# The last expert's tail in a one-core decoder layer: the final weight piece cut by rows, its products in a row, its sums and stores on two engines

## The chip, the cores and the metric

The kernel runs on one core of a Trainium2 chip, as one program from one launch. The metric is the device time in microseconds (us), the median of the runs. The engines are named TensorE (PE in the profile, PEld for its weight loads), VectorE (DVE), ScalarE (ACT), GpSimd (POOL) and SyncE (SP). SyncE issues nearly all DMAs here.

## The reference, cut to what matters

The layer is an RMS norm, one input projection, a state-space mixer and a stick-breaking attention side by side, their merge, an output projection and a residual add; then a mixture of 32 experts over 256 tokens of width 2048. All of it is fp32. The change lies in the last expert of the mixture:

```
D_MODEL = 2048; SEQ = 256; N_EXPERTS = 32; D_FF_EXPERT = 512
# top-1 group of 8 experts, top-2 experts in it; combine[token, e] is the gate, 0 where not chosen
for e in range(N_EXPERTS):
    hid = jax.nn.silu(t @ w_gate[e]) * (t @ w_up[e])
    out = out + combine[:, e:e + 1] * (hid @ w_down[e])
return x + out
```

## The kernel before, in words

After the first part (projection, mixers, merge, router) the experts are worked through, four to a group q (eight groups). Each expert has 32 slots for tokens. `gather` selects the tokens of the four experts by a one-hot matrix (128 slots), `gate_up` computes gate and up products and the transposed hidden activations `hT` of one expert, `down` multiplies them by the down weights, and `scatter` brings the four experts' results back to the tokens and adds them to `accv`, a tile of 128 x 2 x 2048 in SBUF: t = 0 and 1 are the two halves of the 256 tokens, n = 0 to 3 the four quarters of 512 columns.

An expert's weights come in six pieces of 2 MiB, each a tile `ew` of 128 rows by 4096 numbers: four pieces of gate and up (`wgu`), two of down (`wd`; piece 4 for the output columns 0 to 1023, piece 5 for 1024 to 2047). `load_piece` (line 867) issues them on SyncE's queue in the order of `pieces`, into a ring of buffers, well ahead of their use. For experts 30 and 31 the order is changed: all of their gate and up pieces, then (30,4), (31,4), (30,5), (31,5). The last, (31,5), is loaded in two halves of its columns (`LSPLIT` = 512, line 883), so that the first half can be used while the second is on its way.

`down(e, hT, dn, c0, cw)` (line 1137) makes `cw` output columns from `c0` on: matmuls with 32 slots as rows, four column groups of the array at a time, into a PSUM tile `dn`, and then four copies by ScalarE into `Y4` (rows 32i to 32i+31 for expert i of the group; `Y4` is a part of the tile shown as XY). `scatter(q, n, ts)` (line 1152) takes, for each t, a PSUM tile, one matmul of `SC` (the gates, transposed; shown as sc) with `Y4`, one VectorE add into `accv`, and in the last group a store of that part of the output by SyncE. A matmul of fp32 shows as two entries in the trace for 128x512.

The program's order is the order in the code (a manual schedule), engine by engine; waits between engines are semaphores put in by the framework. PSUM tiles come from three pools: `acc` with four banks, `bga` and `bgb` with two each. `keep_busy(n)` issues n transposes into an `acc` tile that nobody reads.

Behind the last store is a loop over experts with more than 32 tokens (line 1198); in the run shown its body isn't entered. All engines read its count (`oli`) and branch over the body.

The tail, in order (lines 1174 to 1189): `gate_up` of experts 30 and 31, `down` of both for columns 0 to 1023, `scatter` of n = 0 and 1, `down` of 30 for 1024 to 2047, `down` of 31 for 1024 to 1535, `scatter` of n = 2 for t = 0, `down` of 31 for 1536 to 2047, `scatter` of n = 2 for t = 1, and of n = 3.

Of the kernel before, what the change touches and what calls it, by code (L numbers as in the profile page):

```python
# [13 lines left out]
OP = mybir.AluOpType  # L14
# [3 lines left out]
P = 128  # L18
# [19 lines left out]
TAILB = (24, 24, 0, 0)  # L38
LSPLIT = 512
# [43 lines left out]
def hybrid_block(ctx, tc, A, out):  # L83
    nc = tc.nc
    load = {"vec": 0.0, "act": 0.0, "pe": 0.0}
    vec = Meter(nc.vector, load, "vec")
    act = Meter(nc.scalar, load, "act")
    pe = Meter(nc.tensor, load, "pe")
    sp, pool = nc.sync, nc.gpsimd
# [3 lines left out]
    def unit(i, shape, dt, name):  # L93
        return U[i].tile(shape, dt, name=name, tag="u")
# [13 lines left out]
    def acc_tile(name="acc"):  # L108
        return pacc.tile([P, 512], F32, name=name, tag="acc")

    def bg_tile(k):
        return pbg.tile([P, 512], F32, name="bg" + "ab"[k], tag="bg" + "ab"[k])
# [46 lines left out]
    ident = cp.tile([P, P], F32, name="ident")  # L159
# [109 lines left out]
    S = {}  # L269
# [137 lines left out]
    for b, s in turns:  # L407
        src, nk, begin, mm, fin = blocks[b]
# [452 lines left out]
    pieces = [(e, i) for e in range(NE - 2) for i in range(6)]  # L861
# [5 lines left out]
    def load_piece():  # L867
        n = nextp[0]
        if n >= len(pieces):
            return  # L870
        j = n % 11 if n < 22 else (n - 22) % 10
        j += n >= 22 and j > 5
        if used[0] <= held.get(j, -1):
            return
        held[j] = n
        e, i = pieces[n]
        tl = ring[j].tile([P, 4, 1024], F32, name="ew", tag="u")
        src = A["wgu"][e][:, 4 * i:4 * i + 4] if i < 4 else A["wd"][e][:, 4 * i - 16:4 * i - 12]
        if n < 7:
            for k in range(4):  # L880
                ahead.append(lambda k=k: sp.dma_start(tl[:, k], src[:, k]))
        else:
            for c0, cw in (((0, 1024),) if n < len(pieces) - 1 else ((0, LSPLIT), (LSPLIT, 1024 - LSPLIT))):
                sp.dma_start(tl[:, :, c0:c0 + cw], src[:, :, c0:c0 + cw])
        ptile[e, i] = tl
        nextp[0] += 1

# [30 lines left out]
    for i in range(nsub):  # L918
        prog["step"] = i
        src, s, nk, begin, mm, fin = subs[i]  # L920
# [14 lines left out]
        for g in (gens[:1] if i < HOLD else list(gens)):  # L935
            while rest.get(g, 0) <= i:
                if load["pe"] > pe0 + BURST or load["vec"] > load["pe"] + SLACK or load["act"] > load["pe"] + SLACK:
                    break
                c = next(g, None)
# [13 lines left out]
        if i >= first_out - X2_AT - 8 and (i % 2 == 0 or 0 <= i - first_out + X2_AT < 4):  # L953
            if not ahead and nextp[0] < 7:
                load_piece()
            if ahead:
                ahead.pop(0)()
        if i == nsub - 4:
            load_piece()
# [10 lines left out]
    def keep_busy(n):  # L970
        ps = acc_tile()
        for _ in range(n):
            pe.transpose(ps[:, 0:P], ident, ident)
# [90 lines left out]
    Y4 = XY[:, 1].rearrange("p a b -> p (a b)")  # L1064


    SC = [None, None]
# [41 lines left out]
    def gate_up(e, gen):  # L1109
        q, i = divmod(e, 4)  # L1110
        gu = acc_tile()
        for k4 in range(4):
            next(gen, None)
            if k4 == (1 if e == 0 else 0):
                next(gen, None)
            if e >= NE - 2:
                keep_busy(24)
            w = ptile[e, k4]
            for kk in range(4):
                k = 4 * k4 + kk  # L1120
                for j in range(4):
                    pe.matmul(gu[32 * j:32 * j + 32, 0:T], XB[:, k, 32 * i:32 * i + 32], w[:, kk, T * j:T * j + T],
                              start=(k == 0), stop=(k == 15), tile_position=(0, 32 * j))
            used[0] += 1
            load_piece()
        for _ in gen:
            pass
        sg = rt.tile([P, P], F32, name="sg", tag=f"sg{e % 2}")
        act.activation(sg, gu[:, 0:P], AF.Silu)
        vec.tensor_tensor(sg, sg, gu[:, P:T], op=OP.mult)  # L1130
        ht = bg_tile(1)
        pe.transpose(ht[:, 0:P], sg, ident)
        hT = rt.tile([P, P], F32, name="hT", tag=f"hT{e % 2}")
        act.copy(hT, ht[:, 0:P])
        return hT

    def down(e, hT, dn, c0, cw):
        i = e % 4
        w = ptile[e, 4 + c0 // 1024]
        n4 = cw // 4  # L1140
        for j in range(4):
            for c in range(4):
                x0 = c0 % 1024 + n4 * c
                pe.matmul(dn[32 * c:32 * c + 32, c0 // 4:c0 // 4 + n4], hT[:, 32 * j:32 * j + 32],
                          w[:, j, x0:x0 + n4], start=(j == 0), stop=(j == 3), tile_position=(0, 32 * c))
        if (c0 + cw) % 1024 == 0:
            used[0] += 1
            load_piece()
        for c in range(4):
            act.copy(Y4[32 * i:32 * i + 32, c0 + n4 * c:c0 + n4 * c + n4], dn[32 * c:32 * c + 32, c0 // 4:c0 // 4 + n4])  # L1150

    def scatter(q, n, ts=(0, 1)):
        if q == 0 and n == 0:
            S["acc"] = unit(3, [P, 2, D], F32, "accv")
        accv = S["acc"]
        c = slice(512 * n, 512 * n + 512)
        for t in ts:
            ps = acc_tile()
            pe.matmul(ps, SC[q % 2][:, P * t:P * t + P], Y4[:, c], start=True, stop=True)
            vec.tensor_tensor(accv[:, t, c], (x2 if q == 0 else accv)[:, t, c], ps, op=OP.add)  # L1160
            if q == NE // 4 - 1:
                sp.dma_start(out[t][:, c], accv[:, t, c])
# [3 lines left out]
    for e in range(NE - 2):  # L1166
        hT = gate_up(e, gather(e // 4) if e % 4 == 0 else iter(()))
        dn = acc_tile()
        for c0 in (0, 1024):
            down(e, hT, dn, c0, 1024)  # L1170
            if e % 4 == 3:
                for n in range(c0 // 512, c0 // 512 + 2):
                    scatter(e // 4, n)
    pair = [(e, gate_up(e, iter(())), acc_tile()) for e in (NE - 2, NE - 1)]
    q = NE // 4 - 1
    keep_busy(TAILB[0])
    down(*pair[0], 0, 1024)
    keep_busy(TAILB[1])
    down(*pair[1], 0, 1024)
    scatter(q, 0)  # L1180
    scatter(q, 1)
    keep_busy(TAILB[2])
    down(*pair[0], 1024, 1024)
    keep_busy(TAILB[3])
    down(*pair[1], 1024, LSPLIT)
    scatter(q, 2, (0,))
    down(*pair[1], 1024 + LSPLIT, 1024 - LSPLIT)
    scatter(q, 2, (1,))
    scatter(q, 3)


    accv = S["acc"]
# [5 lines left out]
    with tc.For_i(0, novr) as it:  # L1198
        er = nc.values_load(oli[0:1, bass.ds(it + 1, 1)], min_val=0, max_val=NE - 1)
        gp = [acc_tile() for _ in range(4)]  # L1200
        for k4 in range(4):
# [8 lines left out]
            for i in range(4):  # L1210
                k = 4 * k4 + i
                for t in range(2):
                    for hf in range(2):
                        pe.matmul(gp[2 * t + hf], XO[:, k, P * t:P * t + P], WO[k4][:, i, 512 * hf:512 * hf + 512],
                                  start=(k == 0), stop=(k == 15))
# [12 lines left out]
        for t in range(2):  # L1228
            for n in range(4):
                ps = acc_tile()  # L1230
                for j in range(4):
                    pe.matmul(ps, hOT[:, j, P * t:P * t + P], WO[n // 2][:, j, 512 * (n % 2):512 * (n % 2) + 512],
                              start=(j == 0), stop=(j == 3))
                c = slice(512 * n, 512 * n + 512)
# [56 lines left out]
```

## Time and profile before

| what | value |
|---|---|
| median of 3 runs | 1557.23 us (1555.97 to 1557.52) |
| the profiled execution, its own time | 1555.73 us |
| its span (first to last instruction) | 1553.9 us |
| mean granted TensorE clock | 0.923 of full |
| PE busy | 1252.9 us (81%) |
| PEld busy | 856.7 us (55%) |
| DVE busy | 540.5 us (35%) |
| ACT busy | 451.1 us (29%) |
| DMA | 516.91 MB, mean 333 GB/s |

Times in the rows are us from the start of the span unless marked ns. A timeline row gives the start, the time from the first start to the last end, engine, line, operation, out<-in, shapes and xcount, and in brackets the idle time before it with what ended it. Because of a helper that records every operation, all compute rows have line 77; the tiles tell them apart. Matmuls overlap, so a row of several is shorter than their sum, and the ends of matmuls are modelled. In the rows by stretch the columns are: the stretch, its length, then for PE, PEld, DVE, ACT and POOL the busy us and (x) the number of instructions, then the granted TensorE clock as a share, the busy share of the 16 DMA engines and GB/s. A name with a q (SPq, PEldq) is an engine's sequencer, which waits, branches and issues DMAs.

### The profile page before, as it was taken

To read this page: it belongs to the slowest core of one execution; us is meant where nothing else is said; L and a number is where in the kernel's file an instruction comes from. 1 tells how busy PE (TensorE), PEld (TensorE's weight loads), DVE (VectorE), ACT (ScalarE), POOL (GpSimd) and SP (SyncE) were. 2 spreads that over 40 slices of the span, in tenths; PEclk is the share of its full clock that TensorE was granted. 3 is DMA by queue.
4 is the path that set the end of the run, shared out by engine and by line. 5 is a ranking of instruction groups with operands and counts; after the bars stand their busy time and mean duration, and the time that the engine had idled before them with its cause. 6 is when DMAs were issued, how large, how long until landed. Compare 5 with 4: busy or idle time off the path is not lost. (4 is left out here: it accounts for less than half of the span.)

```text
span 1553.9 us, 25147 instructions
## 1 busy us (share of the span) xinstructions
PE 1252.9 (81%) x10662; PEld 856.7 (55%) x10662; DVE 540.5 (35%) x1344; ACT 451.1 (29%) x768; POOL 48.1 (3%) x105
## 2 busy tenths in 40 slices
PE   9999999999999999878558558557657657656697
PEld 8888888888878888644224224224223324323364
DVE  6746788898866744302002002002002002002001
ACT  5654577544454444121101100110110110110101
POOL 6500000000000000000000000000000000000000
PEclk9999999999999999999789779888888889879899
DMA  7645555566658877999999999999999999999996
GB/s 259 200 148 161 178 163 162 162 191 191 190 189 287 273 270 245 382 427 428 427 426 428 426 427 427 427 427 428 426 428 427 427 427 427 427 427 427 427 427 259
DMA packets 65108, 516.91 MB, mean 333 GB/s; under 512 B 7905, under 2 KB 8161, under 8 KB 41441
## 3 DMA queue, kind: packets, MB, share of 16 engines
q1 hardware_dynamic: 64704, 515.21, 84.4%
q8 instruction: 86, 1.41, 0.4%
q14 instruction: 30, 0.24, 0.0%
q10 hardware_dynamic: 288, 0.06, 0.0%
HBM read 513.14 MB, written 2.10 MB: 332 GB/s over the span
## 5 line engine op out<-in xcount | busy, mean ns | idle before, releaser
L77 PE MATMUL acc<-ew,XY 128*32 128x256 f32 x4096 | 309.1, 455 | 169.9 <-DMA ew<-wgu 169.8
L77 PEld LDWEIGHTS acc<-ew,XY 128*32 128x32 f32 x4096 | 142.3, 126 | 320.7 <-DMA ew<-wgu 189.1
L77 DVE TENSOR_TENSOR wl<-raw,wh 128x1024 fp32r<-128x1024 f32 (+1 forms) x201 | 244.1, 1217 | 140.6 <-ACT wh L77 139.3
L77 ACT CAST wh<-raw 128x1024 fp32r<-128x1024 f32 x199 | 208.6, 1053 | 179.0 <-PE acc L77 113.7
L77 DVE TENSOR_TENSOR sg<-sg,acc 128x128 f32<-128x128 f32 x32 | 9.2, 288 | 660.2 <-ACT sg L77 660.2
L77 PE MATMUL acc<-ew,hT 128*32 128x256 f32 (+1 forms) x2080 | 149.2, 436 | 71.3 <-DMA ew<-wd 39.4
L77 ACT COPY XY<-acc 32x256 f32<-32x256 f32 (+1 forms) x260 | 93.7, 360 | 209.8 <-PE acc L77 207.3
L77 PEld LDWEIGHTS acc<-ew,hT 128*32 128x32 f32 x2080 | 73.6, 123 | 138.3 <-issue 54.8
L77 PE MATMUL acc<-wh,xh 128*128 128x512 f32 x512 | 144.8, 399 | 1.1 <-DVE wh L77 0.8
L77 PE MATMUL acc<-wh,xl 128*128 128x512 f32 x512 | 140.3, 391 | 0.0
L77 PE MATMUL acc<-wl,xh 128*128 128x512 f32 x512 | 140.0, 390 | 0.0
L77 ACT ACTIVATE sg<-acc 128x128 f32<-128x128 f32 x32 | 8.9, 278 | 416.0 <-PE acc L77 416.0
L77 PEld LDWEIGHTS acc<-wh,xl 128*128 128x128 f32 x512 | 96.6, 189 | 20.6
L77 PEld LDWEIGHTS acc<-wl,xh 128*128 128x128 f32 x512 | 96.5, 189 | 20.3
L77 PEld LDWEIGHTS acc<-wh,xh 128*128 128x128 f32 x512 | 93.4, 189 | 20.2 <-issue 1.2
L77 DVE TENSOR_TENSOR Vs<-Vs,prod 128x32 f32<-128x32 f32 x508 | 76.9, 222 | 0.0
L77 PE MATMUL acc<-XY,sc 128*128 128x512 f32 x128 | 61.9, 624 | 14.7 <-ACT XY L77 14.5
L77 PE MATMUL bga<-SL,x 128*128 128x128 f32 x512 | 63.5, 280 | 10.3 <-DVE SL L77 10.3
L77 PEld LDWEIGHTS bga<-SL,x 128*128 128x128 f32 x512 | 59.0, 192 | 22.9 <-DVE SL L77 15.9
L77 DVE TENSOR_TENSOR accv<-accv,acc 128x512 f32<-128x512 f32 x56 | 38.5, 688 | 79.9 <-PE acc L77 79.9
L77 PE MATMUL acc<-wh,m 128*128 128x512 f32 x256 | 64.6, 392 | 0.0
L77 DVE TENSOR_TENSOR prod<-Vs,coef 128x64 f32<-128x64 f32 x254 | 56.1, 263 | 0.0
(222 smaller groups left out, 972.5 us busy)
## 6 DMA issues: line engine op xcount, KB each, us to landing
ew<-wgu SPq DMA_DIRECT2D x123, 2048.0 KB, 39.3
ew<-wd SPq DMA_DIRECT2D x61, 2048.0 KB, 39.4
raw<-win SPq DMA_DIRECT2D x127, 512.0 KB, 4.2
raw<-wout SPq DMA_DIRECT2D x32, 512.0 KB, 4.2
ew<-wgu SPq DMA_DIRECT2D x20, 512.0 KB, 5.6
raw<-wba SPq DMA_DIRECT2D x16, 512.0 KB, 4.5
raw<-wbs SPq DMA_DIRECT2D x16, 512.0 KB, 4.8
raw<-wglu SPq DMA_DIRECT2D x8, 512.0 KB, 5.5
```

Source lines behind the costliest of these rows:

```text
L77: return f(out, *args, **kw)
```

## The change

The last weight piece is loaded as rows 0 to 119 and rows 120 to 127, over all its columns, instead of as two column halves. The tail after `scatter` of n = 1 is rewritten. `down` of expert 30 is as it was. Then, for n = 2 and 3, a tile `ends[n, 1]` is opened in PSUM with a matmul of the identity and `accv[:, 1]`, which puts the sum so far of the second token half there. The two products of expert 31 (512 columns each) follow in a row; the first goes into its tile as before and is copied by VectorE, the second goes into another tile and is copied by ScalarE. Last come four scatter matmuls. For t = 0 VectorE adds the result to `accv` and SyncE stores it; for t = 1 the matmul adds onto what the identity matmul left in PSUM, ScalarE copies it to `accv`, and ScalarE's own queue stores it. The two calls of `keep_busy` that go were of length 0.

```diff
         else:
-            for c0, cw in (((0, 1024),) if n < len(pieces) - 1 else ((0, LSPLIT), (LSPLIT, 1024 - LSPLIT))):
-                sp.dma_start(tl[:, :, c0:c0 + cw], src[:, :, c0:c0 + cw])
+
+            for r in ((slice(0, P),) if n < len(pieces) - 1 else (slice(0, 120), slice(120, P))):
+                sp.dma_start(tl[r], src[r])
...
-    def down(e, hT, dn, c0, cw):
+    def down(e, hT, dn, c0, cw, copy=act.copy):
...
-            act.copy(Y4[32 * i:32 * i + 32, c0 + n4 * c:c0 + n4 * c + n4], dn[32 * c:32 * c + 32, c0 // 4:c0 // 4 + n4])
+            copy(Y4[32 * i:32 * i + 32, c0 + n4 * c:c0 + n4 * c + n4], dn[32 * c:32 * c + 32, c0 // 4:c0 // 4 + n4])
...
-    keep_busy(TAILB[2])
     down(*pair[0], 1024, 1024)
-    keep_busy(TAILB[3])
-    down(*pair[1], 1024, LSPLIT)
-    scatter(q, 2, (0,))
-    down(*pair[1], 1024 + LSPLIT, 1024 - LSPLIT)
-    scatter(q, 2, (1,))
-    scatter(q, 3)
+
+    accv = S["acc"]
+    ends = {}
+    for n in (2, 3):
+        ends[n, 0] = bg_tile(0)
+        ends[n, 1] = acc_tile()
+        pe.matmul(ends[n, 1], ident, accv[:, 1, 512 * n:512 * n + 512], start=True, stop=False)
+    e, hT, dn = pair[1]
+    down(e, hT, dn, 1024, 512, vec.tensor_copy)
+    down(e, hT, acc_tile(), 1536, 512)
+    for n in (2, 3):
+        c = slice(512 * n, 512 * n + 512)
+        for t in range(2):
+            pe.matmul(ends[n, t], SC[q % 2][:, P * t:P * t + P], Y4[:, c], start=not t, stop=True)
+            if t:
+                act.copy(accv[:, t, c], ends[n, t])
+                nc.scalar.dma_start(out[t][:, c], accv[:, t, c])
+            else:
+                vec.tensor_tensor(accv[:, t, c], accv[:, t, c], ends[n, t], op=OP.add)
+                sp.dma_start(out[t][:, c], accv[:, t, c])
```

TensorE at the end of the program, before: the row of 32x256 is `down` of expert 30, the rows of 32x128 are expert 31, the rows `acc<-XY,sc` are scatter matmuls; what an instruction waits for stands in brackets (DMAHW is a load's landing).

```order
L77 MATMUL acc<-ew,hT 32x256 x15
L77 MATMUL acc<-ew,hT 32x128 [waits DMAHW4_49]
L77 MATMUL acc<-ew,hT 32x128 x15
L77 MATMUL acc<-XY,sc 128x512 [waits DVE_49,Activation_49]
L77 MATMUL acc<-ew,hT 32x128 [waits DMAHW5_49]
L77 MATMUL acc<-ew,hT 32x128 x15
L77 MATMUL acc<-XY,sc 128x512 [waits DVE_49]
L77 MATMUL acc<-XY,sc 128x512 [waits Activation_49]
L77 MATMUL acc<-XY,sc 128x512 [waits DVE_49]
```

The same place now, with the identity matmuls as `acc<-accv,ident`:

```order
L77 MATMUL acc<-ew,hT 32x256 x15
L77 MATMUL acc<-accv,ident 128x512 [waits DVE_49] x2
L77 MATMUL acc<-ew,hT 32x128 [waits DMAHW5_49,DMAHW4_49]
L77 MATMUL acc<-ew,hT 32x128 x15
L77 MATMUL acc<-ew,hT 32x128 [waits Activation_49]
L77 MATMUL acc<-ew,hT 32x128 x15
L77 MATMUL bga<-XY,sc 128x512 [waits DVE_49]
L77 MATMUL acc<-XY,sc 128x512
L77 MATMUL bga<-XY,sc 128x512 [waits Activation_49]
L77 MATMUL acc<-XY,sc 128x512
```

Both products of expert 31 have moved ahead of every scatter matmul of n = 2 and 3, two identity matmuls stand before them, and the first of them waits for both loads.

ScalarE at the end of the program now, from its copies for expert 30 on (32x256); before, eight copies of 32x128 stood between these and the read of `oli`:

```order
L77 COPY XY<-acc 32x256 x3
L77 COPY XY<-acc 32x128 [waits PE_49]
L77 COPY XY<-acc 32x128 x3
L77 COPY accv<-acc 128x512 [waits DMAHW5_49,DMAHW3_49,DMAHW6_49,DMAHW0_49,PE_49]
L1200 DMA out<-accv 128x512 [waits DMAHW3_49,Activation_49]
L77 COPY accv<-acc 128x512 [waits PE_49]
L1200 DMA out<-accv 128x512 [waits DMAHW5_49,Activation_49]
L1211 TENSOR_LOAD oli [waits DVE_49]
```

Four of the small copies have gone to VectorE, and two large copies and two stores have come to ScalarE ahead of its read of `oli`; VectorE has two adds fewer in turn.

## Rows read from the trace of the kernel before

**Rows 1.** Chain of waits in order of time: start, us, what.
```profile
1545.19 2.00 PE acc L77 x4
...
1547.21 0.69 DVE accv L77
```
**Rows 2.** Busy time by stretch; columns as described in the section on the profile.
```profile
1500.00:1520.00 20.00, 19.10 (x230) 14.58 (x229) 0.29 (x1) 0.54 (x2) 0.00 (x0) 1.00 1.01 427
...
1531.00:1532.00 1.00, 1.00 (x27) 0.73 (x20) 0.00 (x0) 0.00 (x0) 0.00 (x0) 1.00 0.50 213
...
1542.00:1543.00 1.00, 1.00 (x6) 0.24 (x10) 0.00 (x0) 0.00 (x0) 0.00 (x0) 1.00 0.19 57
```
**Rows 3.** Timeline of SP, issues: piece before the last, second half of the last.
```profile
1495.91 0.33 SPq L884 DMA_DIRECT2D ew<-wd  x1
...
1505.64 7.34 SPq L884 DMA_DIRECT2D ew<-wd  x1
```
**Rows 4.** DMA issues, the same two in order: xcount, KB, us to landing.
```profile
ew<-wd SPq DMA_DIRECT2D x1, 2048.0 KB, 39.4
...
ew<-wd SPq DMA_DIRECT2D x1, 1024.0 KB, 34.9
```
**Rows 5.** Timeline of PE from expert 30's second down product on (the first two overlap).
```profile
1537.27 1.93 PE L77 MATMUL acc<-ew,hT 128*32 128x256 f32 x32
...
1537.27 2.81 PE L77 MATMUL acc<-ew,hT 128*32 128x256 f32 x64
1541.88 1.12 PE L77 MATMUL acc<-XY,sc 128*128 128x512 f32 x2 [1.80 <-ACT XY L77]
1542.93 1.08 PE L77 MATMUL acc<-ew,hT 128*32 128x128 f32 x32
1543.94 3.23 PE L77 MATMUL acc<-XY,sc 128*128 128x512 f32 x6
...
1545.19 1.98 PE L77 MATMUL acc<-XY,sc 128*128 128x512 f32 x4
```
**Rows 6.** Timeline of ACT, the copies for expert 31's two halves.
```profile
1540.77 1.06 ACT L77 COPY XY<-acc 32x128 f32<-32x128 f32 x4
...
1544.08 1.06 ACT L77 COPY XY<-acc 32x128 f32<-32x128 f32 x4 [2.26 <-PE acc L77]
```
**Rows 7.** Timeline of DVE, three of the last group's eight adds.
```profile
1537.37 0.69 DVE L77 TENSOR_TENSOR accv<-accv,acc 128x512 f32<-128x512 f32 x1 [0.17 <-PE acc L77]
...
1546.36 0.69 DVE L77 TENSOR_TENSOR accv<-accv,acc 128x512 f32<-128x512 f32 x1 [0.56 <-PE acc L77]
1547.21 0.69 DVE L77 TENSOR_TENSOR accv<-accv,acc 128x512 f32<-128x512 f32 x1 [0.17 <-PE acc L77]
```
**Rows 8.** Groups of instructions by form: count | busy us, mean ns | idle before.
```profile
L77 ACT COPY xt<-bga 128x512 f32<-128x512 f32 x8 | 4.7, 583 | 17.8 <-PE bga L77 17.8
...
L77 DVE TENSOR_TENSOR sg<-sg,acc 128x128 f32<-128x128 f32 x32 | 9.2, 288 | 660.2 <-ACT sg L77 660.2
...
L77 DVE COPY OV<-bgb 32x1 f32<-32x1 f32 x1 | 0.1, 147 | 0.1
```
**Rows 9.** Timeline: the last store's issue on SP; an issue on ACT.
```profile
1547.93 0.33 SPq L1162 DMA_DIRECT2D out<-accv  x1
...
1.09 0.43 ACTq L425 DMA_DIRECT2D g<-g  x1
```
**Rows 10.** DMA issues, the store of 1543.75 and the last: KB, us to landing.
```profile
out<-accv SPq DMA_DIRECT2D x1, 256.0 KB, 2.5
...
out<-accv SPq DMA_DIRECT2D x1, 256.0 KB, 4.1
```
**Rows 11.** Line 1198, the branch and its waits: ns min/median/max, first and last start.
```profile
L1198 PEldq COMPARE_BRANCH  x1: 4417/4417/4417, 1547.5 to 1547.5; - x1
...
L1198 SPq EVENT_SEMAPHORE  x2: 17/17/17, 1552.0 to 1552.1; - x2
...
L1198 ACTq COMPARE_BRANCH  x3: 38/38/54, 1544.7 to 1552.4; - x3
```

## The prediction

> **What bounds the kernel now.** I read the stretches of the span first. The whole second half is paced by loading: 427 GB/s with every DMA engine busy [rows 2], and this change leaves all of that alone. It touches the last load and what follows it, so only the last 20 us of 1553.9 are at stake. The chain of waits, read next, ends in four matmuls and one add into accv at 1547.21 [rows 1]; behind them stand the last store and the end of the program.
>
> The last loads: the piece before the last is issued at 1495.91 and lands 39.4 us later, at 1535.3; the second half of the last piece goes out at 1505.64 and lands after 34.9, at 1540.5 [rows 3, 4]. From 1531 on the loads run at half the rate (share 0.50, 213 GB/s) [rows 2]: half of the DMA engines are done, the other half carries the tail.
>
> On TensorE [rows 5], `down` of expert 30 (32 matmuls of 256 columns) starts at 1537.27, 2.0 us after its weights landed, since the previous sums stood before it. The first half of expert 31 follows directly (x64, 2.81 us). Then TensorE idles until 1541.88, 1.80 us, for ScalarE, whose last four copies start at 1540.77 [rows 6]. So the order is: one sum, the second half of `down` at 1542.93 (2.4 us after its weights), ScalarE's copies at 1544.08, and sums from 1545.19. What ends last here is the ping-pong of TensorE and ScalarE, and not the DMA. [...]
>
> Behind the last add (1547.21 + 0.69 = 1547.90) two things run side by side. The last store is issued at 1547.93 and lands 4.1 us later, at 1552.0, where an earlier one took 2.5 [rows 9, 10]. TensorE's branch over the overflow loop starts at 1547.5 and takes 4.417 us, to 1551.9; SyncE's wait for the landing ends at 1552.0 [rows 11]. Both end together, and 1.9 us of closing follow.
>
> **The change part by part.**
>
> *120 and 8 rows.* One DMA engine's share of a 2 MiB piece takes 2.097 MB / 427 GB/s = 4.91 us [rows 2], so a last piece in whole rows is in at 1535.3 + 4.91 = 1540.2 if the 120 rows spread evenly, against 1540.5. One more row on a late engine costs 4.91 / 8 = 0.61 us, which gives 1540.8. I keep both. What is lost is the early half: both products now wait for the whole piece, behind which the rest of TensorE's work is queued.
> [...]
>
> *Two identity matmuls of accv.* A product of 128x512 is two entries; from the pair at 1541.88 to the next work at 1542.93 are 1.05 us, and a second pair adds 1.98 - 1.12 = 0.86, in all 1.91 [rows 5]. They begin when `down` of expert 30 is through: 1537.27 + 2.81 - 1.08 = 1539.00. Their two banks were read by VectorE's adds, the last at 1537.37 + 0.69 = 1538.06 [rows 7], so they do not wait. They end at 1540.91. Cost: 1.91 us of TensorE, but they stand where it idles now and cover the load (1540.2 to 1540.8). That cover is thin: a load later than 1540.8 is paid in full.
>
> *Products in a row, two banks.* The first 32 matmuls of expert 31 now start at 1540.91, not 1539.00; the second 32 follow 2.81 - 1.93 = 0.88 later [rows 5], at 1541.79 instead of 1542.93. TensorE is through with them 1.01 after that (1542.93 to 1543.94), at 1542.80.
>
> *Copies by two engines.* A copy starts 1.15 us after the first of its 32 matmuls (1542.93 to 1544.08) [rows 5, 6]. VectorE thus begins at 1542.06. No row has a VectorE copy of 32x128 out of PSUM: a copy of 32x1 takes 147 ns, an operation of 128x128 on PSUM 288 [rows 8]; ScalarE's takes 1.06 / 4 = 265. I take 250, nearest to these last: four are 1.0 us, to 1543.06 (bounds 1542.65 and 1543.21). ScalarE starts the other four at 1542.94 and ends at 1544.00.
>
> *The four sums.* They start 0.05 after the copies (1545.14 to 1545.19), at 1543.11; bounds 1542.80, where TensorE gets free, and 1543.26. The third needs ScalarE's copies (1544.00), but its turn comes at 1544.9. A sum is there 1.17 after its start (1545.19 to 1546.36), each further one 0.85 later (to 1547.21) [rows 5, 7]. The last is there at 1543.11 + 1.17 + 3 x 0.855 = 1546.85, against 1547.21: **0.36 us earlier** (0.21 to 0.67). The gain is small because four sums now stand behind the last copies where two did: they start 2.08 earlier, and the two more give 1.71 back.
>
> *Half of the adds in PSUM.* For t=1, ScalarE's copy of 128x512 (583 ns) stands in for VectorE's add (0.69) [rows 7, 8]. Last copy: 1546.85 + 0.58 = 1547.43 against 1547.90, 0.47 earlier.
>
> *Two store queues.* An issue holds SyncE 0.33 us, and one on ScalarE took 0.43 [rows 9]; the results come 0.85 apart, so no store waits for another's issue and I count nothing. ScalarE's first copy into accv also waits for two loads and for two of the first four stores; their adds were over by 1538.06 [rows 7], some 7 us before, so I count nothing there either. Its register load and branch move behind its last issue, to about 1547.9, ahead of TensorE's end.
>
> *The end.* TensorE's branch moves by the same 0.36: 1547.5 - 0.36 + 4.42 = 1551.6. The last store lands at 1547.46 + 2.5 = 1550.0, or 1551.6 if it is held as now (4.1). Either way the end moves by 0.36. The profiled execution took 1555.73, 1.83 beyond its span; it becomes 1555.4. The median of the three runs, 1557.23, lies 1.5 above it, and on that I put the forecast: **1556.9 us**. That is 0.02%; less than 0.2%, some 3.1 us, can't be told from no change here.
>
> **The rivals.**
>
> *The 120 rows spread badly (slower).* No transfer of before has a row count other than 128. If the 120 rows go to eight engines, 15 each, and those are the late ones, with one of the 8 rows on top, their queue ends at 1535.3 + 16 x 0.61 = 1545.1. TensorE, free at 1540.9, waits for 4.2 us of it, since both products need all rows; less the 0.36 that is +3.8: 1561.0. It decides from a landing after 1540.9, and shows above 0.2% from one after 1544.4. For it: half of the engines do run late. Against it: if the eight are the early half, done by 1531, nothing is lost. Chance 0.06.
> [...]
>
> *TensorE's branch gets short, or the store's delay goes (faster than forecast).* The 4.417 us are one event, and ScalarE's branch at the same line takes 38 to 54 ns [rows 11]. If TensorE's vanishes, the store at 1550.0 ends the kernel, 2.0 earlier: 1555.2. The loop body that it jumps over is unchanged, which speaks against it. Chance 0.08.
>
> *ScalarE becomes the last.* It now issues the last store and branches after it. Should its branch take what TensorE's does, 1547.43 + 0.43 + 4.42 = 1552.3, 0.4 later than TensorE's 1551.9 now, and its register load comes on top: about +0.7, 1557.9. Before, its branch takes 38 to 54 ns [rows 11], so 0.08.
>
> **How the numbers follow.** The forecast has 0.78. Its own range is 1556.6 to 1557.0 by the bounds, and 1555.3 to 1557.6 with the spread of the runs (1555.97 to 1557.52). Low end: the short branch with a fast run, 1554.9; high end: the ScalarE case with a slow one, 1558.6. What is left out is the bad spread and runs off in either direction. Slower by over 0.2%: 0.06 of the first rival and 0.01 of drift; faster by that much: no case reaches it, 0.03 for drift; within 0.2%: 0.90.
>
> **What would show it.** Identity matmuls right behind `down` of expert 30, before 1539.1; no wait on DMA at the 64 matmuls of expert 31; VectorE copies of about 250 ns; the four sums in a row without a gap, the last 3.7 us after the first starts; TensorE's branch again some 4.4 us long and within 0.2 us of the last landing. I am wrong if TensorE waits for the last piece, if the VectorE copies take over 300 ns, or if another wait closes the program.

## The result, and the profile after

The changed kernel takes 1567.16 us (median of 4 runs, 1565.35 to 1569.55) against 1556.69 us: ratio 1.0066, 95% interval 1.0054 to 1.0079. It is slower by about 10.5 us, where the prediction said no change (1556.9). The profiled execution took 1567.27 us with a span of 1565.6 (before: 1555.73 and 1553.9).

The stretches of the span, columns as in [rows 2], show it first:

```profile
1500.00:1520.00 20.00, 18.97 (x230) 14.38 (x227) 0.29 (x1) 0.55 (x2) 0.00 (x0) 1.00 1.01 426
...
1527.00:1534.00 7.00, 5.61 (x67) 4.64 (x66) 0.00 (x0) 1.45 (x4) 0.00 (x0) 1.00 0.95 211
...
1539.00:1543.00 4.00, 3.16 (x33) 1.29 (x25) 0.00 (x0) 0.81 (x3) 0.00 (x0) 0.50 0.51 135
...
1545.00:1547.00 2.00, 2.00 (x4) 0.77 (x3) 0.93 (x2) 0.00 (x0) 0.00 (x0) 0.50 0.56 193
```

From 1500 to 1520 us the rate is as before (426 GB/s with all engines busy). From 1527 to 1534 the DMA engines are still busy (0.95) but move half as much, 211 GB/s. In [rows 2] a rate of 213 came with a share of 0.50: there half of the engines were done, here all work at half speed. A packet of these loads is 16,384 B in the trace (one row), so 16 engines x that x share / rate is the time of one: 0.62 us at first, 1.18 us here. The trace's own records of these packets have the same means, 0.62 and 1.18 us.

The issues of the first down piece of expert 31, still 128 rows, and of the 120 rows (KB, us to landing):

```profile
ew<-wd SPq DMA_DIRECT2D x1, 2048.0 KB, 45.1
...
ew<-wd SPq DMA_DIRECT2D x1, 1920.0 KB, 48.9
```

The first is issued at 1493.22 and lands at 1538.3; a whole piece took 39.4 in [rows 4]. The 120 rows, issued at 1503.01, land at 1551.95. So a load that the change does not touch, two places ahead of the one that it does, is late as well. TensorE's timeline tells which of the two is paid for:

```profile
1529.87 1.93 PE L77 MATMUL acc<-ew,hT 128*32 128x256 f32 x32 [1.39 <-DMA ew<-wd]
1531.73 2.84 PE L77 MATMUL acc<-ident 128*128 128x128 f32 x24
1538.45 3.64 PE L77 MATMUL acc<-ew,hT 128*32 128x256 f32 x32 [3.88 <-DMA ew<-wd]
1542.94 5.83 PE L77 MATMUL acc<-XY,sc 128*128 128x512 f32 x8 [0.84 <-ACT XY L77]
1548.70 1.93 PE L77 MATMUL acc<-ew,hT 128*32 128x256 f32 x32
1550.56 1.98 PE L77 MATMUL acc<-accv,ident 128*128 128x512 f32 x4
1552.47 1.95 PE L77 MATMUL acc<-ew,hT 128*32 128x128 f32 x64
1554.94 1.13 PE L77 MATMUL bga<-XY,sc 128*128 128x512 f32 x2 [0.51 <-DVE XY L77]
...
1557.62 1.02 PE L77 MATMUL acc<-XY,sc 128*128 128x512 f32 x2
```

TensorE waits 1.39 and 3.88 us for the first down pieces of experts 30 and 31, neither of which is split. In the second wait, which no work of TensorE fills, its granted clock falls from 1.00 to 0.50, and it is still there from 1545 to 1547: the 32 matmuls take 3.64 where the same number took 1.93, the eight entries of the sums 5.83. At the 64 products of the split piece it does not wait: they follow the identity matmuls at 1552.47, and the load had landed 0.5 us before. The chain of waits ends accordingly (start, us, what):

```profile
1493.22 45.10 DMA ew<-wd
1538.45 3.68 PE acc L77 x32
1542.94 10.66 PE acc L77 x76
```

The new tail, on VectorE and then on ScalarE, and the branch over the overflow loop (line 1212 now):

```profile
1553.69 1.20 DVE L77 COPY XY<-acc 32x128 f32<-32x128 f32 x4 [4.20 <-PE acc L77]
```
```profile
1554.50 1.06 ACT L77 COPY XY<-acc 32x128 f32<-32x128 f32 x4 [2.31 <-PE acc L77]
...
1558.68 0.59 ACT L77 COPY accv<-acc 128x512 f32<-128x512 f32 x1 [1.13 <-PE acc L77]
1559.30 0.35 ACTq L1200 DMA_DIRECT2D out<-accv  x1
```
```profile
L1212 PEldq COMPARE_BRANCH  x3: 97/197/4232, 1556.3 to 1564.1; - x3
```

```profile
L77 DVE COPY XY<-acc 32x128 f32<-32x128 f32 x4 | 1.2, 289 | 4.2 <-PE acc L77 4.2
```

VectorE's four copies take 289 ns each, and 1.20 us from the first start to the last end; TensorE's branch is long again (4232 ns, 4417 in [rows 11]).

### The profile page after: what moved, and what is told of

It reads as the page before. It is cut to its first block, busy times and chain, and to the rows that moved or that the text cites. A ratio compares the mean times of both kernels' runs of the same rounds, so it can differ in the third digit from the quotient of the medians.

```text
span 1565.6 us, 25158 instructions
## 1 busy us (share of the span) xinstructions
PE 1264.1 (81%) x10666; PEld 859.4 (55%) x10666; DVE 540.2 (35%) x1346; ACT 451.1 (29%) x766; POOL 48.6 (3%) x105
## 4 chain that ended last, share of the span: by engine, by line
DMA 53%; PE 44%; DVE 2%; ACT 1%; issue 0%; SPq 0%; DVEq 0%; ACTq 0%
PE acc L77 38%; DMA ew<-wgu 35%; DMA ew<-wd 18%; PE bga L77 4%; PE bgb L77 2%; DVE R L77 0%; DMA raw<-win 0%; DVE wl L77 0%; ACT XY L77 0%; ACT wh L77 0%; DVE Vs L77 0%; ACT AT L77 0%; DVE prod L77 0%; DVE XY L77 0%; ACT gate L77 0%
## 5 line engine op out<-in xcount | busy, mean ns | idle before, releaser
L77 PE MATMUL acc<-ew,XY 128*32 128x256 f32 x4096 | 316.4, 463 | 172.1 <-DMA ew<-wgu 171.9
```

Of the source, the lines that this page charges most:

```text
L77: return f(out, *args, **kw)
```

## The experiments

Theory A: the time of a packet hangs on which rows the DMA engines write at the same time. A load of 120, 64, 16 or 8 neighbouring rows hands its rows out to the engines otherwise than one of 128 (the trace has 15 increments for the 120 rows, 8 for the 8 rows and 16 for a whole piece); engines then hinder each other in writing, and all that do, those still in an ordinary load too, slow down from the 0.62 us of a packet to 1.18. Half of the engines run some 10 us behind the others (for the first down piece of expert 30, in the kernel before, eight increments came by 1516.2 and the last at 1525.6), so the early ones reach the 120 rows while the late ones are two pieces back. Up to here no run shows that the rows written matter; A supposes it.

Rival B: an odd number of engines, 15 for the 120 rows, slows the load. The other rivals are described where they come up.

**The change in parts.** Four kernels, two of them the changed kernel without the row split:

```
e1: for c0 in (0, 512): sp.dma_start(tl[:, :, c0:c0+512], src[:, :, c0:c0+512])   # last piece, rest as after
e2: for r in (slice(0, 120), slice(120, P)): sp.dma_start(tl[r], src[r])          # last piece, rest as before
e3: sp.dma_start(tl, src)                                                         # last piece, rest as after
e4: for r in (slice(0, 64), slice(64, P)): sp.dma_start(tl[r], src[r])            # last piece, rest as after
```

e1. 

> The changed kernel, with only the last piece's load put back to two column halves of all 128 rows. [...] Rival E (the new order of the tail, both products behind the whole piece, costs the time and the late landing is its result): 1566 to 1568 us as with the change.

e2. 

> The kernel before, with only the last piece loaded as 120 and 8 rows; order of the tail, copies and stores as before. Theory A: the packets double from the moment when the first engines reach the 120 rows, the last landing slips by 9 to 11 us, and the time is 1566 to 1569 us. Rival B: the same. Rival E: within 1 us of 1557 us.

e3. 

> The changed kernel, with the last piece in one load of 128 rows. Theory A: packets stay at 0.61 us, the landing is at 1540.2 to 1540.6 us, and this is the case that my prediction worked out: 1556 to 1557 us. Rival C (the small extra transfer of 8 rows is to blame, queued behind the large one): the same. Rival E: 1566 to 1568 us.

e4. 

> The changed kernel, with the last piece as two loads of 64 rows. The number of engines is then even and each has four rows of each load. [...] Rival B (15 engines, one left out) and rival C (a short last transfer of 8 rows): 1556 to 1558 us, packets 0.61 us.

Measured against the kernel before (1558.09): e1 1558.19 us, ratio 0.9999 (0.9990 to 1.0008); e2 1571.63, 1.0079 (1.0060 to 1.0098); e3 1558.44, 1.0000 (0.9991 to 1.0009); e4 1567.22, 1.0059 (1.0044 to 1.0075). Within the 1.5 us or so to which these times are known, the new tail costs nothing and gains nothing; the row split alone, in the old kernel, costs all of it and more (E falls). 64 and 64 rows, with an even count and no short transfer, cost nearly as much (B and C fall). Two sizes missed: e3 lies above 1556 to 1557, as e1 and the kernel before do in this series, and e2 lies above 1566 to 1569, for its 120 rows landed 51.7 us after their issue (1555.5), 12 us more than the 39.4 of a whole piece in [rows 4], where I had 9 to 11. The rate of e2, then of e4:

```profile
1527.00:1534.00 7.00, 5.19 (x63) 4.21 (x61) 0.00 (x0) 0.91 (x4) 0.00 (x0) 1.00 0.95 194
```
```profile
1527.00:1533.00 6.00, 5.05 (x60) 3.84 (x58) 0.00 (x0) 1.45 (x4) 0.00 (x0) 1.00 1.02 232
```

Packets thus of 1.28 and 1.15 us. In e2 TensorE does wait for the split piece, which lands 3.6 us later than in the changed kernel, with no identity matmuls ahead of its products:

```profile
1539.42 3.52 PE L77 MATMUL acc<-ew,hT 128*32 128x256 f32 x32 [3.48 <-DMA ew<-wd]
...
1555.59 1.93 PE L77 MATMUL acc<-ew,hT 128*32 128x128 f32 x32 [5.99 <-DMA ew<-wd]
```

e3 is the case that the prediction worked out, and it serves for the sum of the profiled executions, for its first down piece of expert 30 is issued at 1487.67 as in the changed kernel. Its TensorE:

```profile
1532.68 1.93 PE L77 MATMUL acc<-ew,hT 128*32 128x256 f32 x32
1535.46 3.95 PE L77 MATMUL acc<-XY,sc 128*128 128x512 f32 x8 [0.84 <-ACT XY L77]
1539.34 1.93 PE L77 MATMUL acc<-ew,hT 128*32 128x256 f32 x32
1541.21 1.99 PE L77 MATMUL acc<-accv,ident 128*128 128x512 f32 x4
1543.12 1.95 PE L77 MATMUL acc<-ew,hT 128*32 128x128 f32 x64
1545.59 1.12 PE L77 MATMUL bga<-XY,sc 128*128 128x512 f32 x2 [0.52 <-DVE XY L77]
...
1548.27 1.02 PE L77 MATMUL acc<-XY,sc 128*128 128x512 f32 x2
```

Its span is 1556.3, the changed kernel's 1565.6: 9.3 us. The first product of expert 31 starts 5.77 later there (1538.45 against 1532.68, the late pieces), its matmuls and the sums behind it take (3.64 - 1.93) + (5.83 - 3.95) = 3.59 more at the lower clock. That makes 9.36.

**Twelve pieces in the middle.** In the kernel before, one down piece of every second expert is loaded in another form:

```
if n % 12 == 4 and 28 <= n <= 160:
    f1: rows 0:120, then 120:128      f2: columns 0:512, then 512:1024     f7: rows 0:64, then 64:128
    f3: 8 loads, tl[16*j:16*j+16] <- src[16*j:16*j+16]
    f4: 8 loads, tl[j::8]         <- src[16*j:16*j+16]
    f5: 8 loads, tl[:, k, c0:c0+512] <- src[:, k, c0:c0+512]
    f6: 1 load,  tl <- src.rearrange("(a b) k c -> b a k c", b=8)
```

f1. 

> The kernel before, with 12 pieces in the middle (one down piece of every second expert) loaded as 120 and 8 rows. [...] Rival F (only the tail suffers, since the loads run dry there or the stores are beside them): within 10 us of 1557.

f2. 

> Control for the last: the same 12 pieces as two column halves of 128 rows each, two transfers as well, with packets of 2 KB. Theory A: every engine keeps its rows, packets are not slowed, at most 0.25 us a piece: 1557 to 1561 us. Rival C (the second transfer of a piece costs the time): as with 120 and 8 rows.

f3. 

> The kernel before, with the same 12 pieces loaded as eight transfers of 16 rows, each to 16 rows that follow each other. [...] Rival D (the cost is on the reading side, or in the count of rows, and not in where they are written): the same as the next run, whatever it is.

f4. 

> As the last, from the same rows of memory in the same eight transfers of 16 rows, but written to every eighth row of the tile (so the weights of these pieces stand in other rows than they should). [...] Rival D: no difference between the two.

f5. 

> Control for the runs with eight transfers: the same 12 pieces as eight transfers of 128 rows with 512 columns each. Theory A: packets of 2 KB cost 84 to 86 ns each, eight of them 0.69 us for 0.61, so 0.5 to 1 us a piece: 1562 to 1570 us. Rival C (many transfers cost the time): 90 us or more, as with eight transfers of 16 rows.

f6. 

> The kernel before; the same 12 pieces in one transfer of 128 rows, written to the rows as ever but read from the rows of memory in another order (row 16b+a from row 8a+b; so the weights of these pieces stand in other rows than they should). [...] Rival D (the read side: engines that read neighbouring rows disturb each other): 60 to 160 us more, as with 120 and 8 rows. [...]

f7. 

> The kernel before, with the same 12 pieces as two transfers of 64 rows. [...] Rival B (an engine left out, short transfers of 8 rows): within 10 us of the control with column halves (1564 us).

| run | us | ratio (95%) | us a piece |
|---|---|---|---|
| f1, 120 + 8 rows | 1717.0 | 1.1033 (1.0982 to 1.1084) | 13.2 |
| f7, 64 + 64 rows | 1707.8 | 1.0962 (1.0888 to 1.1037) | 12.5 |
| f3, 8 x 16 neighbours | 1688.5 | 1.0839 (1.0807 to 1.0871) | 10.9 |
| f4, 8 x 16, every eighth | 1649.5 | 1.0585 (1.0567 to 1.0602) | 7.6 |
| f6, read in another order | 1822.1 | 1.1627 (1.1585 to 1.1669) | 22.0 |
| f2, 2 column halves | 1563.9 | 1.0037 (1.0024 to 1.0049) | 0.5 |
| f5, 8 x 512 columns | 1563.8 | 1.0037 (1.0023 to 1.0051) | 0.5 |

The last column is the difference of the medians (1558.0) through 12. The runs of f7 spread most, from 1668.7 to 1730.8 us; the lowest is the one traced, and by it a piece costs 9.2 us. Column pieces cost 0.5 us however many (C falls again; f2's bound of 0.25 us a piece was too low), row pieces 8 to 13, in the middle as at the end (F falls). Two things fit badly. Packets of twice the time make a piece 4.9 us longer, or 9.8 if the early and the late half of the engines come to it one after the other (an estimate from 2.097 MB / 427 GB/s = 4.9 us a piece); f1 costs 13.2. The trace has each engine's increment: those of the 8 rows came 6.4 us apart in the first of the twelve pieces (739.2 to 745.7) and 36.5 in the last (1510.6 to 1547.1), so the engines drift further apart; that this is the rest of the price is argued, not shown. TensorE's clock is lower in f1 as well (0.75 for 0.85 from 720 to 1440 us), but it does not set the pace, for the DMA engines are busy all the time in both kernels and move 358 GB/s in f1 for 427 before (before, then f1):

```profile
720.00:1440.00 720.00, 467.94 (x5221) 239.04 (x5223) 65.52 (x123) 85.08 (x246) 0.00 (x0) 0.85 1.01 427
```
```profile
720.00:1440.00 720.00, 416.11 (x4230) 202.03 (x4230) 50.06 (x96) 69.28 (x201) 0.00 (x0) 0.75 1.00 358
```

And f3, with neighbouring rows, is worse than f4, with every eighth, by 39 us in all, where D had no difference, but in a stretch with both in such a piece (f3, then f4) packets take 1.30 and 1.21 us:

```profile
795.00:808.00 13.00, 5.05 (x64) 2.17 (x56) 0.00 (x0) 0.00 (x0) 0.00 (x0) 0.68 0.95 192
```
```profile
795.00:808.00 13.00, 5.11 (x45) 1.74 (x37) 0.29 (x1) 0.54 (x2) 0.00 (x0) 0.69 0.96 208
```

f6 was to tell reading from writing and did not: its pieces came with eight increments, so eight engines carried 16 rows each, and the number of engines changed together with the order of reading. It left D open.

**Only the rows written differ.** Of the same 12 pieces rows 0 to 63, in eight loads of 8 rows, which go to eight engines; g1 writes each to neighbouring rows, g2 to rows four apart. That engines writing rows four apart leave each other alone, as A has it for g2, no run had shown before:

```
pool.memset(tl[64:], 0.0)
g1: for j in range(8): sp.dma_start(tl[8*j:8*j+8], src[8*j:8*j+8])
g2: for j in range(8): r = 32*(j//4) + j%4; sp.dma_start(tl[r:r+29:4], src[8*j:8*j+8])
```

g1. 

> The kernel before; of the same 12 pieces only rows 0 to 63 are loaded, as eight transfers of 8 rows, each to 8 neighbouring rows (the other 64 rows are set to 0 by GpSimd, so the weights of these pieces are wrong). Each transfer goes to eight engines. [...] Rival D (reading side, row count, number of engines): the same as the next run.

g2. 

> [...] Theory A: packets stay at 0.61 us, eight engines take 4.9 us a piece as ever and the other eight nothing: 1550 to 1570 us. Rival D: as the run with neighbouring rows.

g1 took 1628.28 us, ratio 1.0438 (1.0403 to 1.0472), 5.9 us a piece; g2 1558.26, ratio 1.0005 (0.9995 to 1.0015). A stretch inside such a piece, g1 and then g2, where only the eight engines or little more are busy:

```profile
921.00:927.00 6.00, 0.71 (x8) 0.40 (x12) 0.00 (x0) 0.00 (x0) 0.00 (x0) 0.68 0.49 104
```
```profile
906.00:909.00 3.00, 0.88 (x16) 0.61 (x20) 0.00 (x0) 0.00 (x0) 0.00 (x0) 0.97 0.58 246
```

A share of 0.49 moves 104 GB/s, one of 0.58 moves 246: packets of 1.24 and 0.62 us. Reads, transfers, row count and number of engines are the same, so what slows these loads is where the rows are written, and D falls for them. That the same slows 120 and 8 or 64 and 64 rows is argued from this: no run changed only the rows that those loads write. How engines hinder each other no run shows. The increments of one transfer come 7.2 us apart in g1 (926.3 to 933.6), so its engines are not all in the same transfer at once; how many hinder each other at a time is not settled.

## Why the prediction was wrong

**The failed step is the term "120 and 8 rows".** It priced the load by bytes over rate and by rows per engine (1540.2, or 1540.8 with one row more) and took the rate as given, with the sentence that the change "leaves all of that alone". Measured: 1551.95. The rate was what failed: as one load of 128 rows (e3) the piece landed 4.9 us behind the one before it (1537.4 to 1542.3), just as the term has it, while with rows 0 to 119 loaded by themselves packets took twice as long, those of the other loads in flight too (45.1 us to landing for 39.4). In g1 and g2 it is the rows written that decide the rate; for the 120 rows the same is argued.

In the term the split was worth 0.6 us at most (1540.8 for 1540.2, one more row on a late engine); the changed kernel is 10.5 us slower, and with 64 and 64 rows it takes 8.8 more than in one load (1567.22 for 1558.44).

**The first rival** had the direction, and neither the mechanism nor the place. It gave the 120 rows to eight engines with 15 each, and charged a wait for the split piece, +3.8. The increments in the trace are 15 for the 120 rows and 8 for the 8 rows; what is paid is waits at two untouched pieces (5.3 us) and the lower clock behind the longer one (3.6 us). The sign to look for, "no wait on DMA at the 64 matmuls of expert 31", came true in a kernel that was 10 us slower, by luck: TensorE came to these products late itself, 0.5 us behind the landing.

**Identity matmuls**: from their start to the products 1.91 us in e3 (1541.21 to 1543.12), as worked out; they did cover the load in e3, and in the changed kernel only because TensorE came to them 9.4 us later (1550.56 for 1541.21).

**Copies by two engines**: VectorE's four took 1.20 us where I took 1.0, beyond my upper bound (4 x 288 ns, 1.15): each took 289 ns for my 250, with some 15 ns between them that the sum left out. They started 1.22 behind their products for 1.15.

**The four sums**: the last result stands 3.74 us behind the first start (1554.94 to 1558.68), as predicted. The tail in e3 is nevertheless 0.41 late by my own steps: 0.14 since the products start 3.78 after `down` of expert 30 for 3.64, 0.07 for the copies' start, 0.20 for their length. Counted from that `down` (1539.34 against 1537.27 in [rows 5]), ScalarE's last copy in e3 ends at 1549.33 + 0.59 - 2.07 = 1547.85, where the last add ended at 1547.90 [rows 7]. That copy in e3's timeline of ScalarE:

```profile
1549.33 0.59 ACT L77 COPY accv<-acc 128x512 f32<-128x512 f32 x1 [1.13 <-PE acc L77]
```

That is 0.05 us earlier, where the prediction had 0.47: of the gain of 0.36 next to nothing was left, and the times of e1 and e3, known to some 1.5 us, could not show it.

**Two queues and the end**: ScalarE's issue took 0.35 (I took 0.43), and no store waited. The last one landed 4.0 us after its issue, and TensorE's branch took 4.23 us, so both rivals about the end fall: the branch did not get short, and ScalarE's stayed at 38 to 54 ns.

## What to carry to other kernels

Split a load by columns and leave its 128 rows together; here loads of 120, 64 or 16 rows doubled the time of packets (1.15 to 1.30 us for 0.62), and the loads beside them were late too, in the changed kernel one two pieces ahead (45.1 us to landing for 39.4); two column halves cost 0.5 us a piece. When a transfer changes shape, ask which rows each engine writes, not only how many bytes each has. And where the loads slip, look for the wait that is paid: it may stand at an untouched piece, with the clock that falls behind it as part of the bill (0.50, and 3.6 of 9.4 us here).

## What the runs showed of the hardware that I had not expected

- Packets of 16 KB took 0.62 us in loads of 128 rows, and 1.15 to 1.30 us in the stretches shown with 120 and 8, 64 and 64, and eight times 16 rows.
- Eight engines wrote to rows four apart at full speed each (0.58 of the engines, 246 GB/s, 0.62 us a packet), and to eight neighbouring rows at half of it (1.24 us), so short transfers as such are not slow.
- The 16 engines are not in step: of the first down piece of expert 30, in the kernel before, eight increments came from 1513.8 to 1516.2 and the last at 1525.6.
- One piece in row pieces (f1, f3, f4, f7) cost 8 to 13 us in the middle of the stream, more than the 4.9 us that the piece itself takes.
